# RWKV chunks of two heads: column tiles and half-array products against side-by-side operands and block-diagonal matrices on the whole array

## The chip, the cores and the metric

The kernel runs on one core of a Trainium2 chip. The metric is the device time of one execution in microseconds (us), as a median of several runs. One execution of the kernel before was profiled; every row shown below comes from it. PE is TensorE's matmul stream and PEld its weight loads, DVE is VectorE, ACT ScalarE, POOL GpSimd, and SP the engine that issues most DMAs.

## The reference, cut to what matters

Two layers, each of a mixer, a cross-attention over a memory of 256 rows, and a mixture of 16 experts, on 256 tokens of width 1024, all in f32. The change touches one half of the mixer, the RWKV-7 recurrence with 8 heads of width 64:

```python
def step(state, inp):
    r_t, w_t, k_t, v_t, kk_t, a_t = inp
    sa = jnp.einsum('bhvk,bhk->bhv', state, -kk_t)
    state = (state * w_t[:, :, None, :]
             + sa[..., None] * (kk_t * a_t)[:, :, None, :]
             + v_t[..., None] * k_t[:, :, None, :])
    return state, jnp.einsum('bhvk,bhk->bhv', state, r_t)
...
_, y = lax.scan(step, s0, (time_major(r_h), time_major(w_h), time_major(k_h),
                           time_major(v_h), time_major(kk), time_major(a_h)))
```

The other half of the mixer is a retention over 4 heads, and there are two gates; both need the products of x with columns of one large matrix `w_in`.

## The kernel before

**Chunks.** The recurrence is computed in 4 chunks of 64 tokens. Within a chunk it is a triangular system: a 64x64 matrix of each head and chunk is inverted (`invert`, all 16 of a half at once, on DVE; two levels of products on TensorE then grow 16x16 blocks to 64x64), and from chunk to chunk only the state goes on. The 8 heads lie as 4 pairs, head E of a pair on partitions 0 to 63 and head O on 64 to 127. A layer does two halves (`hf` 0 and 1) one after the other, and each half two pairs in lockstep. So there are 4 halves, 8 pairs and 32 pair-chunks in the program.

**A pair's steps** (`rwkv_pair`, a generator that gives way at each `yield`): (1) DVE and POOL write the operands `stk` (L841, L842) and `bk` (L844, L845); (2) four chunk products a head, `bk` times `stk` (L854), masked by DVE into `mb` and `stk` (L855, L856), and a DMA of the left half of `mb` to `blkin`; then the inversion; (3) the inverse `St` comes back by DMA and goes through the two levels (L876 to L892); (4) the four chunks in a row, each with three dependent stages:

```python
self.mm(pg[h, :], stk[o][:, n, 0:64], sv[o][:, n, :], True, True)
self.mm(pu[h, :], st[h, n, :], gg[h, :], True, True)
self.mm(pd[h, :], bkr[:, n, h], uv[o][:, n, :], True, True)
self.mm(pq[h, :], sv[o][:, n, :], stk[o][:, n, 64:128], True, False)
self.mm(pq[h, :], uv[o][h, n, :], mb[h, n, 64:128], False, True)
```

Each of these lines runs once for head E and once for head O. The results of the two heads go to the two partition halves of one PSUM tile, so the products with 128 rows of operands are column tiles (128x64 of the array), those with 64 rows are quadrants (64x64). DVE copies `pg` to `gg` (L919, one copy for both heads) and `pu` to `uv` (L925, one a head), makes the next state `sv` from `pd` (L932, one a head); ACT copies `pq` to `kk` (L938). Below, stretch A is the run of these four chunks in the first half of layer 0, B in its second half, C and D the same two of layer 1.

**What lies around it.** `filler` holds the products of x with `w_in` for retention and gates; `FILL` says how many of its steps are issued after each step of the pairs, none after the chunks begin. A scheduler then orders the instructions of each engine by its own model of time, so such products also stand between those of the chunks. In the trace they are `acc<-wh,xT` (512 columns) and `acc<-xT,wh` (256 columns), on the whole array. Their weights come by DMA to a ring of buffers, and are split into a high and a low part by ACT (L135) and DVE (L136). After the pairs, what is left of the filler is finished, and the outputs are projected. All matmuls go through `mm` and all transposes through `tr`, so they have L127 and L131 in the trace. An f32 matmul is two instructions there; names such as `rk<-stkE,svE` tell which operands it read, the moving one first in some rows and the stationary one in others. Tiles of one tag share its buffers: `bk` has two, one for each pair of a half.

Of the kernel before, what the change touches and what calls it, by code (L numbers as in the profile page):

```python
# [111 lines left out]
def DQ(nc):  # L112
    return nc.sync


class Build:
# [709 lines left out]
    def rwkv_pair(self, rw, pair, kk, al, k, r, v, P, Pm, Pi):  # L826
# [4 lines left out]
        def T(name, n, bufs=2):  # L831
            return rw.tile([128, 4, n], F32, name=name, bufs=bufs)
# [5 lines left out]
        stk = [T("stkE", 128), T("stkO", 128)]  # L838
        bk = T("bk", 128)
        for o, h in enumerate(half):  # L840
            nc.vector.scalar_tensor_tensor(out=stk[o][h, :, 0:64], in0=ch(kk)[h], scalar=-1.0, in1=ch(Pm)[h], op0=OP.mult, op1=OP.mult)  # L841
            nc.gpsimd.tensor_mul(out=stk[o][h, :, 64:128], in0=ch(r)[h], in1=ch(P)[h])  # L842
            b0, k0 = (0, 64) if o == 0 else (64, 0)
            nc.vector.tensor_mul(out=bk[h, :, b0:b0 + 64], in0=ch(al)[h], in1=ch(Pi)[h])  # L844
            nc.vector.tensor_mul(out=bk[h, :, k0:k0 + 64], in0=ch(k)[h], in1=ch(Pi)[h])  # L845
        yield

        mb = T("mb", 128)
        mask = c["rmask"][:, None, :].to_broadcast([128, 4, 128])
        for o, h in enumerate(half):  # L850
            x = half[1 - o]
            ps = self.rk([128, 4, 128])
            for n in range(4):
                self.mm(ps[:, n, :], bk[h, n, :], stk[o][h, n, :], True, True)  # L854
            nc.vector.tensor_mul(out=mb[h], in0=ps[h], in1=mask[h])  # L855
            nc.vector.tensor_mul(out=stk[o][x], in0=ps[x], in1=mask[x])  # L856
# [3 lines left out]
        for o, h in enumerate(half):  # L860
            DQ(nc).dma_start(out=self.matrices(self.blkin, pair, o), in_=mb[h, :, 0:64])
# [7 lines left out]
        mab = mb[:, :, 0:64]  # L869
        tm = [c["tmask"][:, None, i * 64:i * 64 + 64].to_broadcast([128, 4, 64]) for i in range(2)]  # L870
        st, tt = T("St", 64), T("Tt", 64)
        for o, h in enumerate(half):
# [5 lines left out]
        for lv in range(2):  # L878
# [13 lines left out]
            nc.vector.tensor_add(out=flat(st), in0=flat(st), in1=flat(pz[:, 0]))  # L892
            if lv == 0:
# [6 lines left out]
                uv = [T("uvE", 64), T("uvO", 64)]  # L900
                sv = [T("svE", 64), T("svO", 64)]
# [3 lines left out]
                for o, h in enumerate(half):  # L905
                    x = half[1 - o]
                    for cc in range(2):
                        nc.scalar.copy(out=uv[o][x].rearrange("p (q c) v -> p q c v", c=2)[:, :, cc, :],
                                       in_=pt[cc * 64:cc * 64 + 64, :, o * 64:o * 64 + 64])
                    nc.gpsimd.tensor_copy(out=sv[o][x], in_=uv[o][x])  # L910
                    nc.gpsimd.memset(sv[o][h, 0, :], 0.0)

        for n in range(4):
            yield
            pg = self.rk([128, 64])
            for o, h in enumerate(half):
                self.mm(pg[h, :], stk[o][:, n, 0:64], sv[o][:, n, :], True, True)
            gg = rw.tile([128, 64], F32, name="gg", bufs=2)
            nc.vector.tensor_copy(out=gg, in_=pg)  # L919
            yield  # L920
            pu = self.rk([128, 64])
            for h in half:
                self.mm(pu[h, :], st[h, n, :], gg[h, :], True, True)
            for o, h in enumerate(half):
                nc.vector.tensor_copy(out=uv[o][h, n, :], in_=pu[h])  # L925
            yield
            if n < 3:
                pd = self.rk([128, 64])
                for o, h in enumerate(half):
                    self.mm(pd[h, :], bkr[:, n, h], uv[o][:, n, :], True, True)  # L930
                for o, h in enumerate(half):
                    nc.vector.scalar_tensor_tensor(out=sv[o][h, n + 1, :], in0=sv[o][h, n, :], scalar=Pc[h, n], in1=pd[h],  # L932
                                                   op0=OP.mult, op1=OP.add)
            pq = self.rk([128, 64])
            for o, h in enumerate(half):
                self.mm(pq[h, :], sv[o][:, n, :], stk[o][:, n, 64:128], True, False)
                self.mm(pq[h, :], uv[o][h, n, :], mb[h, n, 64:128], False, True)
            nc.scalar.copy(out=kk[:, n * 64:n * 64 + 64], in_=pq)  # L938
# [426 lines left out]
```

## Time and profile before

| | |
|---|---|
| time, median of 3 runs (lowest to highest) | 1326.06 us (1325.94 to 1327.15) |
| time of the profiled execution | 1326.32 us |
| its span, first to last instruction | 1324.5 us |
| PE busy | 1225.4 us, 93% of the span |
| DVE busy | 759.1 us, 57% |
| ACT busy | 494.9 us, 37% |
| POOL busy | 73.0 us, 6% |

The time around the span is 1.8 us. Matmuls are pipelined: one that has started keeps PE "busy" until its result is out, while the next ones start behind it. What a stream of matmuls costs is read from the distance between their starts, not from their durations. In rows of busy time by stretch, the bracketed numbers are instructions, PEclk is the granted clock of TensorE as a share of 2.4 GHz, and the last two columns are the share of time in which the DMA engines moved data and their GB/s.

### The profile page before, as it was taken

Reading aid. Unit: us, or ns where it says so; the run is one execution under the profiler, and the core shown is the slowest. Engines: PE = TensorE matmul, PEld = TensorE weight load, DVE = VectorE, ACT = ScalarE, POOL = GpSimd, SP = SyncE. Lnnn points to the kernel's source line nnn. Section 1 sums busy time; section 2 is a strip of 40 time slices with the busy share of each in tenths; the row PEclk is TensorE's granted clock in tenths of the full one; section 3 lists DMA queues with packets and bytes.
Section 4 is the critical chain, followed back from the end, with each engine's and each line's share of the span. In section 5 each row is a group of like instructions: output and inputs, shape, how many; then the busy total and the mean of one; then the engine's idle time right before and its main releaser. Section 6 shows DMA issues by size and latency. Waiting matters only on the chain. (4 is left out here: it accounts for less than half of the span.)

```text
span 1324.5 us, 20023 instructions
## 1 busy us (share of the span) xinstructions
PE 1225.4 (93%) x7952; PEld 856.1 (65%) x7952; DVE 759.1 (57%) x1518; ACT 494.9 (37%) x785; POOL 73.0 (6%) x125
## 2 busy tenths in 40 slices
PE   7998998998999999999969998989979969999995
PEld 7886687796888844333329976877959854434331
DVE  6588677487557523333366787865775562333335
ACT  4556333253544322322235663332534312232222
POOL 0012221000000000000000103210000000000000
PEclk9999989999999999999989999999999979999997
DMA  9745132198834899999997452231888349999994
GB/s 318 263 148 180 50 97 76 33 323 290 276 127 175 304 398 402 398 397 402 399 341 228 159 179 72 85 96 48 302 291 312 120 166 349 402 396 401 401 396 194
DMA packets 189843, 331.10 MB, mean 250 GB/s; under 512 B 23152, under 2 KB 80880, under 8 KB 188720
## 3 DMA queue, kind: packets, MB, share of 16 engines
q1 hardware_dynamic: 187728, 324.51, 68.2%
q10 hardware_dynamic: 1728, 3.15, 0.7%
q0 software_dynamic: 288, 2.10, 0.4%
q8 instruction: 66, 1.08, 0.3%
q14 instruction: 33, 0.27, 0.1%
HBM read 321.86 MB, written 7.87 MB: 249 GB/s over the span
## 5 line engine op out<-in xcount | busy, mean ns | idle before, releaser
L136 DVE TENSOR_TENSOR wh<-raw,wh 128x1024 fp32r<-128x1024 f32 (+1 forms) x204 | 232.7, 1143 | 111.0 <-ACT wh L135 109.5
L135 ACT CAST wh<-raw 128x1024 fp32r<-128x1024 f32 (+1 forms) x204 | 199.8, 981 | 155.0 <-PE acc L127 138.5
L127 PE MATMUL acc<-xT,wh 128*128 128x256 f32 x1824 | 247.7, 289 | 2.7 <-DVE xT L136 1.6
L127 PEld LDWEIGHTS acc<-xT,wh 128*128 128x128 f32 x1824 | 225.9, 190 | 11.2 <-DVE xT L136 1.9
L1246 ACT COPY low<-g 64x512 f32<-64x512 f32 x128 | 74.2, 580 | 289.4 <-PE g L127 263.5
L127 PE MATMUL g<-raw,xe 128*64 128x512 f32 x688 | 157.7, 598 | 4.5 <-DVE hT L1255 3.4
L127 PE MATMUL acc<-wh,xT 128*128 128x512 f32 x384 | 101.9, 408 | 3.0 <-DVE vg L557 3.0
L127 PEld LDWEIGHTS g<-raw,xe 128*64 128x64 f32 x688 | 46.0, 136 | 90.7 <-issue 79.9
L1247 DVE TENSOR_TENSOR y<-g,low 64x512 f32<-64x512 f32 x64 | 44.1, 689 | 77.0 <-ACT low L1246 75.8
L127 PE MATMUL g<-raw,hT 128*64 128x512 f32 x352 | 81.4, 596 | 5.2 <-DVE hT L1255 2.6
L127 PEld LDWEIGHTS acc<-wh,xT 128*128 128x128 f32 x384 | 70.1, 188 | 21.5 <-DVE vg L557 3.8
L1247 DVE TENSOR_TENSOR us<-g,low 64x512 f32<-64x512 f32 x32 | 22.0, 689 | 94.4 <-ACT low L1246 94.3
L1247 DVE TENSOR_TENSOR act<-g,low 64x512 f32<-64x512 f32 x32 | 22.0, 689 | 75.2 <-ACT low L1246 75.1
L127 PEld LDWEIGHTS g<-raw,hT 128*64 128x64 f32 x352 | 26.1, 137 | 54.6 <-issue 41.7
L127 PE MATMUL acc<-wh,memT 128*128 128x512 f32 x192 | 51.0, 417 | 0.0
L127 PE MATMUL acc<-memT,wh 128*128 128x256 f32 x384 | 46.5, 282 | 1.6 <-DVE wh L136 1.2
L127 PEld LDWEIGHTS acc<-memT,wh 128*128 128x128 f32 x384 | 45.7, 188 | 2.6 <-DVE wh L136 1.7
L127 PE MATMUL acc<-wh,oT 128*128 128x512 f32 x192 | 45.6, 394 | 1.0 <-DVE x L406 0.8
L127 PE MATMUL acc<-wh,mT 128*128 128x512 f32 x192 | 45.7, 397 | 0.7 <-DVE xr L406 0.7
L127 PE MATMUL acc<-ys,wh 128*128 128x256 f32 x384 | 45.1, 279 | 0.0
L127 PEld LDWEIGHTS acc<-ys,wh 128*128 128x128 f32 x384 | 45.0, 188 | 0.0
L127 PEld LDWEIGHTS g<-oh,xs 128*128 128x128 f32 x256 | 33.4, 196 | 17.1 <-issue 11.2
(310 smaller groups left out, 1700.6 us busy)
## 6 DMA issues: line engine op xcount, KB each, us to landing
raw<-in_w_in_dram SPq DMA_DIRECT2D x46, 1024.0 KB, 5.1
raw<-in_moe_w_down_dram SPq DMA_DIRECT2D x44, 1024.0 KB, 14.9
raw<-in_moe_w_gate_dram SPq DMA_DIRECT2D x43, 1024.0 KB, 13.9
raw<-in_moe_w_up_dram SPq DMA_DIRECT2D x43, 1024.0 KB, 13.8
raw<-in_xa_wkv_dram SPq DMA_DIRECT2D x16, 1024.0 KB, 10.2
wh<-in_moe_w_up_dram SPq DMA_DIRECT2D x15, 1024.0 KB, 14.2
A<-in_moe_w_down_dram SPq DMA_DIRECT2D x10, 1024.0 KB, 13.6
A<-in_moe_w_gate_dram SPq DMA_DIRECT2D x9, 1024.0 KB, 13.7
```

The lines of the kernel that those rows point to most:

```text
L127: self.nc.tensor.matmul(out, lhsT, rhs, start=start, stop=stop, skip_group_check=True)
L135: self.nc.scalar.copy(out=hi, in_=src)
L136: (eng or self.nc.vector).tensor_sub(out=lo, in0=src, in1=hi)
L1246: self.nc.scalar.copy(out=low[h], in_=ps[x])
L1247: self.nc.vector.tensor_add(out=out[h], in0=ps[h], in1=low[h])
```

## The change

The operands of the two heads of a pair are laid side by side in one tile each (`stk`, `uv` and `sv` with an index for the head next to the columns). The matrices that had a block for each head in the two partition halves get a column block for each head too, with zeros in the other two blocks: `sd` (from `St`, written by the last add of the second level) and `mrb` (from the right half of `mb`; the left half is now a tile `mab` of its own). Each of the five products of a pair-chunk is then one product of 128 rows and 128 columns of operands for both heads; the blocks of the result that mix heads are not read. So the result lies in two diagonal blocks, and DVE needs two copies for `gg`, ACT two for `kk`; the last add of the second level becomes two, and the mask products of step (2) become three a head instead of two. POOL clears the zero blocks (four memsets a pair). The products of step (2) go head by head for each chunk instead of four of E and then four of O. `sd` shares the tag of `bk`, and `mrb` those of `k` and `r`.

```diff
@@ -828,37 +828,41 @@
         nc, c = self.nc, self.c
         half = [slice(0, 64), slice(64, 128)]
 
-        def T(name, n, bufs=2):
-            return rw.tile([128, 4, n], F32, name=name, bufs=bufs)
+        def T(name, n, bufs=2, tag=None):
+            return rw.tile([128, 4, n], F32, name=name, tag=tag or name, bufs=bufs)
 
         def ch(t):
             return t.rearrange("p (c t) -> p c t", c=4)
 
 
-        stk = [T("stkE", 128), T("stkO", 128)]
+        stk = rw.tile([128, 4, 2, 2, 64], F32, name="stk", bufs=2)
         bk = T("bk", 128)
         for o, h in enumerate(half):
-            nc.vector.scalar_tensor_tensor(out=stk[o][h, :, 0:64], in0=ch(kk)[h], scalar=-1.0, in1=ch(Pm)[h], op0=OP.mult, op1=OP.mult)
-            nc.gpsimd.tensor_mul(out=stk[o][h, :, 64:128], in0=ch(r)[h], in1=ch(P)[h])
+            nc.vector.scalar_tensor_tensor(out=stk[h, :, 0, o, :], in0=ch(kk)[h], scalar=-1.0, in1=ch(Pm)[h], op0=OP.mult, op1=OP.mult)
+            nc.gpsimd.tensor_mul(out=stk[h, :, 1, o, :], in0=ch(r)[h], in1=ch(P)[h])
             b0, k0 = (0, 64) if o == 0 else (64, 0)
             nc.vector.tensor_mul(out=bk[h, :, b0:b0 + 64], in0=ch(al)[h], in1=ch(Pi)[h])
             nc.vector.tensor_mul(out=bk[h, :, k0:k0 + 64], in0=ch(k)[h], in1=ch(Pi)[h])
         yield
 
-        mb = T("mb", 128)
+        mab, mrb = T("mab", 64), T("mrb", 128, 2, "kr"[pair % 2])
+        for o, h in enumerate(half):
+            nc.gpsimd.memset(mrb[h, :, half[1 - o]], 0.0)
         mask = c["rmask"][:, None, :].to_broadcast([128, 4, 128])
+        ps = [self.rk([128, 4, 2, 64]) for _ in half]
+        for n in range(4):
+            for o, h in enumerate(half):
+                self.mm(ps[o][:, n], bk[h, n, :], stk[h, n, :, o, :], True, True)
         for o, h in enumerate(half):
             x = half[1 - o]
-            ps = self.rk([128, 4, 128])
-            for n in range(4):
-                self.mm(ps[:, n, :], bk[h, n, :], stk[o][h, n, :], True, True)
-            nc.vector.tensor_mul(out=mb[h], in0=ps[h], in1=mask[h])
-            nc.vector.tensor_mul(out=stk[o][x], in0=ps[x], in1=mask[x])
+            nc.vector.tensor_mul(out=mab[h], in0=ps[o][h, :, 0], in1=mask[h, :, 0:64])
+            nc.vector.tensor_mul(out=mrb[h, :, h], in0=ps[o][h, :, 1], in1=mask[h, :, 64:128])
+            nc.vector.tensor_mul(out=stk[x, :, :, o, :], in0=ps[o][x], in1=mask[x].rearrange("p c (a t) -> p c a t", a=2))
         Pc = ch(P)[:, :, 63:64]
         bkc = T("bkc", 128, 1)
         nc.gpsimd.tensor_mul(out=bkc, in0=bk, in1=Pc.to_broadcast([128, 4, 128]))
         for o, h in enumerate(half):
-            DQ(nc).dma_start(out=self.matrices(self.blkin, pair, o), in_=mb[h, :, 0:64])
+            DQ(nc).dma_start(out=self.matrices(self.blkin, pair, o), in_=mab[h])
         yield
 
         def per(ps, lhsT, rhs):
@@ -866,9 +870,12 @@
                 for h in half:
                     self.mm(ps[h, n, :], lhsT[h, n, :], rhs[h, n, :], True, True)
 
-        mab = mb[:, :, 0:64]
         tm = [c["tmask"][:, None, i * 64:i * 64 + 64].to_broadcast([128, 4, 64]) for i in range(2)]
         st, tt = T("St", 64), T("Tt", 64)
+
+        sd = T("Sd", 128, 2, "bk")
+        for o, h in enumerate(half):
+            nc.gpsimd.memset(sd[h, :, half[1 - o]], 0.0)
         for o, h in enumerate(half):
             DQ(nc).dma_start(out=st[h], in_=self.matrices(self.blkout, pair, o))
         yield
@@ -889,53 +896,53 @@
             if lv == 0:
                 per(pz[:, 1], st, y)
                 nc.vector.tensor_add(out=flat(tt), in0=flat(tt), in1=flat(pz[:, 1]))
-            nc.vector.tensor_add(out=flat(st), in0=flat(st), in1=flat(pz[:, 0]))
-            if lv == 0:
+                nc.vector.tensor_add(out=flat(st), in0=flat(st), in1=flat(pz[:, 0]))
 
                 bkr = T("bkr", 128)
                 pt = self.rk([128, 4, 128])
                 for n in range(4):
                     self.tr(pt[:, n, :], bkc[:, n, :])
                 nc.scalar.copy(out=flat(bkr), in_=flat(pt))
-                uv = [T("uvE", 64), T("uvO", 64)]
-                sv = [T("svE", 64), T("svO", 64)]
+
+                uv, sv = (rw.tile([128, 4, 2, 64], F32, name=n, bufs=2) for n in ("uv", "sv"))
                 pt = self.rk([128, 2, 128])
                 for i in range(2):
                     self.tr(pt[:, i, :], v[:, i * 128:i * 128 + 128])
                 for o, h in enumerate(half):
                     x = half[1 - o]
                     for cc in range(2):
-                        nc.scalar.copy(out=uv[o][x].rearrange("p (q c) v -> p q c v", c=2)[:, :, cc, :],
+                        nc.scalar.copy(out=uv[x, :, o].rearrange("p (q c) v -> p q c v", c=2)[:, :, cc, :],
                                        in_=pt[cc * 64:cc * 64 + 64, :, o * 64:o * 64 + 64])
-                    nc.gpsimd.tensor_copy(out=sv[o][x], in_=uv[o][x])
-                    nc.gpsimd.memset(sv[o][h, 0, :], 0.0)
+                    nc.gpsimd.tensor_copy(out=sv[x, :, o], in_=uv[x, :, o])
+                    nc.gpsimd.memset(sv[h, 0, o], 0.0)
+            else:
+                for h in half:
+                    nc.vector.tensor_add(out=sd[h, :, h], in0=st[h], in1=pz[h, 0])
 
         for n in range(4):
             yield
-            pg = self.rk([128, 64])
-            for o, h in enumerate(half):
-                self.mm(pg[h, :], stk[o][:, n, 0:64], sv[o][:, n, :], True, True)
+            pg = self.rk([128, 128])
+            self.mm(pg, flat(stk[:, n, 0]), flat(sv[:, n]), True, True)
             gg = rw.tile([128, 64], F32, name="gg", bufs=2)
-            nc.vector.tensor_copy(out=gg, in_=pg)
+            for h in half:
+                nc.vector.tensor_copy(out=gg[h], in_=pg[h, h])
             yield
             pu = self.rk([128, 64])
-            for h in half:
-                self.mm(pu[h, :], st[h, n, :], gg[h, :], True, True)
+            self.mm(pu, sd[:, n, :], gg, True, True)
             for o, h in enumerate(half):
-                nc.vector.tensor_copy(out=uv[o][h, n, :], in_=pu[h])
+                nc.vector.tensor_copy(out=uv[h, n, o], in_=pu[h])
             yield
             if n < 3:
-                pd = self.rk([128, 64])
+                pd = self.rk([128, 128])
+                self.mm(pd, bkr[:, n, :], flat(uv[:, n]), True, True)
                 for o, h in enumerate(half):
-                    self.mm(pd[h, :], bkr[:, n, h], uv[o][:, n, :], True, True)
-                for o, h in enumerate(half):
-                    nc.vector.scalar_tensor_tensor(out=sv[o][h, n + 1, :], in0=sv[o][h, n, :], scalar=Pc[h, n], in1=pd[h],
+                    nc.vector.scalar_tensor_tensor(out=sv[h, n + 1, o], in0=sv[h, n, o], scalar=Pc[h, n], in1=pd[h, h],
                                                    op0=OP.mult, op1=OP.add)
-            pq = self.rk([128, 64])
-            for o, h in enumerate(half):
-                self.mm(pq[h, :], sv[o][:, n, :], stk[o][:, n, 64:128], True, False)
-                self.mm(pq[h, :], uv[o][h, n, :], mb[h, n, 64:128], False, True)
-            nc.scalar.copy(out=kk[:, n * 64:n * 64 + 64], in_=pq)
+            pq = self.rk([128, 128])
+            self.mm(pq, flat(sv[:, n]), flat(stk[:, n, 1]), True, False)
+            self.mm(pq, flat(uv[:, n]), mrb[:, n, :], False, True)
+            for h in half:
+                nc.scalar.copy(out=kk[h, n * 64:n * 64 + 64], in_=pq[h, h])
         yield
```

## Rows read from the trace of the kernel before

**Rows 1.** The page, part 1: busy us, share of the span, instructions.
```profile
PE 1225.4 (93%) x7952; PEld 856.1 (65%) x7952; DVE 759.1 (57%) x1518; ACT 494.9 (37%) x785; POOL 73.0 (6%) x125
```

**Rows 2.** Windows A, between, B, tail, C: length, PE, PEld, DVE, ACT, POOL, PEclk.
```profile
151.04:176.44 25.40, 25.40 (x186) 16.92 (x182) 14.43 (x45) 4.56 (x11) 5.42 (x8) 0.88 0.13 42
176.44:230.92 54.48, 50.04 (x507) 44.95 (x506) 41.84 (x133) 22.11 (x40) 9.18 (x16) 0.96 0.31 91
230.92:253.97 23.05, 23.05 (x197) 16.89 (x193) 11.38 (x40) 4.07 (x10) 0.00 (x0) 1.00 0.08 25
253.97:275.00 21.03, 21.03 (x170) 20.23 (x168) 11.73 (x23) 10.00 (x15) 0.00 (x0) 1.00 0.36 122
818.80:841.91 23.11, 23.11 (x187) 15.44 (x183) 13.21 (x44) 4.56 (x11) 4.75 (x7) 1.00 0.14 46
```

**Rows 3.** Timeline of PE inside stretch A: start us, us, instruction, count.
```profile
157.73 0.33 PE L127 MATMUL rk<-gg,St 64*64 64x64 f32 x4
158.00 0.50 PE L127 MATMUL acc<-wh,xT 128*128 128x512 f32 x1
158.43 0.33 PE L127 MATMUL rk<-gg,St 64*64 64x64 f32 x4
...
159.12 0.27 PE L127 MATMUL rk<-uvE,bkr 128*64 128x64 f32 x1
...
160.26 0.27 PE L127 MATMUL rk<-uvE,bkr 128*64 128x64 f32 x1
```

**Rows 4.** Timeline of PE elsewhere: whole-array products one after another.
```profile
113.94 10.07 PE L127 MATMUL acc<-wh,xT 128*128 128x512 f32 x42 [1.64 <-DVE vg L557]
...
182.52 1.03 PE L127 MATMUL rk<-mixc,sq 128*128 128x2 f32 x8
183.41 0.63 PE L131 MATMUL tp<-cst,rqo 128*128 128x128 f32 x4
183.80 4.83 PE L127 MATMUL acc<-xT,wh 128*128 128x256 f32 x38
...
204.14 0.91 PE L127 MATMUL acc<-vg,rst 128*128 128x128 f32 x6 [1.12 <-DVE rst L589]
```

**Rows 5.** PE groups in A, then in B: filler products among the chunks.
```profile
L127 PE MATMUL acc<-wh,xT 128*128 128x512 f32 x18 | 7.2, 461 | 0.0
L127 PE MATMUL acc<-xT,wh 128*128 128x256 f32 x12 | 4.3, 422 | 0.0
...
L127 PE MATMUL acc<-xT,wh 128*128 128x256 f32 x40 | 10.1, 334 | 0.0
```

**Rows 6.** DVE groups in B: count, busy us, mean ns, idle before.
```profile
L136 DVE TENSOR_TENSOR wh<-raw,wh 128x1024 fp32r<-128x1024 f32 x2 | 2.4, 1224 | 0.1
L925 DVE COPY uvO<-rk 64x64 f32<-64x64 f32 x8 | 1.8, 228 | 0.2
...
L932 DVE SCALAR_TENSOR_TENSOR svO<-svO,P,rk 64x64 f32<-64x64 f32 x6 | 1.7, 287 | 0.2
L919 DVE COPY gg<-rk 128x64 f32<-128x64 f32 x8 | 1.7, 221 | 5.3 <-PE rk L127 5.3
...
L892 DVE TENSOR_TENSOR St<-St,rk 128x256 f32<-128x256 f32 x2 | 0.8, 421 | 0.5 <-PE rk L127 0.5
```

**Rows 7.** Timeline, step (2) of the first half: pair products and first mask.
```profile
94.20 0.82 PE L127 MATMUL rk<-stkE,bk 64*128 64x128 f32 x5
...
96.26 0.68 DVE L855 TENSOR_TENSOR mb<-rk,mixc 64x512 f32<-64x512 f32 x1
```

**Rows 8.** Timeline: operands of the second half, before and at the end of A.
```profile
144.39 1.30 DVE L844 TENSOR_TENSOR bk<-av,cum 64x256 f32<-64x256 f32 x3
...
173.26 0.72 POOL L842 TENSOR_TENSOR stkE<-r,P 64x256 f32<-64x256 f32 x1 [6.19 <-PE rk L127]
173.33 0.93 DVE L841 SCALAR_TENSOR_TENSOR stkE<-kk,sw 64x256 f32<-64x256 f32 x1
```

**Rows 9.** ACT's group of line 938 in layer 0: busy, mean ns, idle.
```profile
L938 ACT COPY kk<-rk 128x64 f32<-128x64 f32 x16 | 3.4, 213 | 37.0 <-PE rk L127 37.0
```

## The prediction

> **What bounds the kernel now.** The page comes first: PE is busy for 93% of the span, DVE for 57% [rows 1]. That is an average, so the stretches that the change touches come next [rows 2]. In A, B and C (and D, which is B again in layer 1) PE never looks idle, and DVE is busy for about half of the time. The stretch between A and B is another matter: PE idles for 54.48 - 50.04 = 4.4 us of it and DVE is busy for 41.8 of 54.5. After B, PE is full again with filler. So what PE gives up in a chunk stretch reaches the end of the mixer, as long as the chunks' own chain does not become longer than PE's work. The weights of later stages don't hold it back: the DMA engines are busy for 0.08 to 0.36 of these stretches.
>
> Is a full PE also a useful PE? That is read from distances between starts, inside A [rows 3]. A filler product of 512 columns that stands alone between two groups of chunk products takes 158.43 - 158.00 = 0.43 us. The same product in a run of 42 takes 10.07 / 42 = 0.24 [rows 4]. So about 0.2 us is lost around each such product, at the places where the array goes from 128x128 to a tiled shape and back. The groups themselves: `pu` of one pair takes 158.00 - 157.73 = 0.27, and `pd` with `pq` 160.26 - 159.12 = 1.14 [rows 3]. `pg` looks like `pu`, so a pair-chunk costs PE 0.27 + 0.27 + 1.14 = 1.68 us, besides what the filler loses.
>
> **Step 1, the chunk products.** They become five per pair-chunk (four in the last chunk, which has no `pd`), each two instructions on the whole array: 2 pairs x (3 x 5 + 4) = 38 products, 76 instructions a stretch. No row shows these very products. Eight whole-array f32 instructions with only two moving columns, and what follows, lie 183.41 - 182.52 = 0.89 apart, so 0.111 each; six with 128 columns take 0.91 with the latency of the last one, so at most 0.15 each [rows 4]. I take 0.111: it leaves those six 0.91 - 5 x 0.111 = 0.35 for the latency of the last one, near the 0.27 of a tiled one [rows 3]. Then the products need 76 x 0.111 = 8.4 us of PE (11.4 at 0.15).
>
> The filler in B is 40 products of 256 columns [rows 5] at 4.83 / 38 = 0.127 [rows 4]: 5.1 us. In A (and C) it is 18 of 512 and 12 of 256 [rows 5]: 18 x 0.24 + 12 x 0.127 = 5.8 us. If no hand-over costs anything once all is of one shape, PE's floor is 13.5 us in B and D and 14.2 in A and C, against 23.1 now [rows 2].
>
> One rule speaks against this step. The rows show what a pair gets from tiles now: the four instructions of a `pu`, two a head, last 0.33 together, though one alone lasts 0.27 [rows 3], so the heads share the array's time. The Trainium skill, "TensorEngine Tiling (Array Packing)", section Theoretical Speedup, says the same in general: operands of at most 64 rows or columns run up to twice as fast as tiles. By it the products alone would get dearer, and the result would be that of the last rival below; by the rows above, the hand-overs that go are worth more. The sum goes by the rows.
>
> But the chunks also have a chain, and it gets longer. DVE's copies of `pg` become two; one of 64 partitions costs as much (0.228) as one of 128 (0.221) [rows 6]. For one pair-chunk DVE then works 0.45 for `gg`, 0.45 for `uv`, 0.56 for `sv`: 1.45 us, and 2.9 for both pairs. Two weight splits of 1.22 a stretch [rows 6] add 0.6 a chunk: 3.5. PE needs 2 x 10 x 0.111 + 5.1/4 = 3.5 a chunk in B, 3.7 in A. One pair alone, never disturbed, needs 3 x (0.111 + 0.35) + 1.45 = 2.8. So PE and DVE tie, and two queues that feed each other in order never both run full. I take 4.2 a chunk, 20% above the tie, and 3.4 for the last one: 16.0 a stretch. Gain 23.1 - 16.0 = 7.1, four times: 28.4 us. Bounds: 37.0 (PE's floor: 2 x 9.6 + 2 x 8.9), and 12.4 if a stretch takes 20, when most chunks wait once for a split of 1.22 on DVE.
>
> **Step 2, the clock.** A holds the same work as C but takes 25.40 against 23.11; the granted clock there is a mean 0.88, in C 1.00 [rows 2]: part of A ran at 1.2 GHz. Whether a denser PE keeps 2.4 GHz is open: 0 to 2.3 us, taken 1.1 gain.
>
> **Step 3, step (2) of the pairs.** The first mask product starts 96.26 - 94.20 = 2.06 us after the first pair product [rows 7]. With E and O alternating, on different rows of the array and different PSUM tiles, sixteen instructions of a pair may overlap two by two: 8 x 0.111 + 0.27 = 1.2, so 0.9 earlier a half; or not at all. The mask products go from four of 0.68 to six (0.43, 0.43, 0.69 a head): +0.36 a pair, 0.7 a half. Both bounds, four halves: -3.6 to +2.9; taken 0.
>
> **Step 4, the evictions that become two.** `sd`: one add of 0.42 [rows 6] becomes two of about 0.42, eight pairs: 3.4 us, before the first `gg` in DVE's queue but beside `pg` and filler on PE: half, +1.7 (0 to 3.4). `kk`: 32 more copies of 0.21 on ACT, which idles for 37.0 us in layer 0 alone before such copies [rows 9]: hidden, but for the last of each half: +0.4 (0 to 0.8). POOL's 32 memsets lie on an engine that is busy for 73 us in all [rows 1]; nothing waits for them but `mrb` and `sd`, whose inputs come later. `uv` and `sv` are written by as many instructions as before, and the DMAs stay two a pair, each of the same size.
>
> **Step 5, a wait that is new.** `sd` lies in the buffers of `bk`, and is read until the last `pu` of a half. Now the second half's `bk` is written before A starts, at 144.4 [rows 8]. After the change it can't be before A's last `pu`: 8 products of 0.43 a layer, 3.5 us, go to the end of A, where the second half's `stk` (L841) already waits its turn at 173.3. DVE's product took 0.93 there beside one of POOL's [rows 8], so up to 8 x 0.93 = 7.4. What queues behind are the pair products and the inversion. PE's cover is `rwkv_out` and filler; DVE has none, since it is busy three quarters of that stretch. Taken +2 a layer: +4 (0 to 14.8). `mrb` in the buffers of `k` and `r` waits for readers of step (1) only, which stand ahead of it in DVE's and POOL's queues: nothing.
>
> **The sum.** -28.4 - 1.1 + 0 + 1.7 + 0.4 + 4 = -23.4. The profiled execution took 1326.3 (span 1324.5 and 1.8 around it): 1302.9. It lies 0.3 above the median of 1326.06: **1302.6 us**.
>
> **Rivals.**
> *PE alone sets the pace.* The scheduler's order happens to keep DVE ahead. For it: A and B now hold one filler product between most groups, which is time in which DVE can finish; against it: DVE is as full as PE. 1326.0 - 37.0 - 1.1 + 1.7 + 0.4 + 0 to 4 = 1290 to 1294; with the clock and step 3 in full, 1285.
> *DVE and the chain set the pace.* A split of 1.22 in front of a copy delays both pairs, and a stretch takes 20: 1326.0 - 12.4 - 1.1 + 6.1 = 1318.6, and 1322 with half of step 5's bound. For it: DVE idles only 5.3 us before `gg` in B [rows 6], and DVE's work grows.
> *It all comes back between A and B.* Step 5 at its bound (14.8) with that last case: 1326.0 - 12.4 - 1.1 + 2.1 + 14.8 = 1329, or no change when the filler covers a part. For it: PE already idles there.
> *Slower: packing is lost and nothing else.* Suppose the 0.2 us around a filler product has to do with waiting for operands, not with the shape. Then the distances of 0.43 stay, and only the array's time grows. The four instructions of a `pu` start within at least 0.33 - 0.27 = 0.06 us of each other [rows 3]; taken as 0.1, a whole-array product of 0.222 costs 0.12 more: 38 x 0.12 = 4.6 a stretch, 18 in all: 1326.0 + 18 + 6 = 1350. It decides from the point where a lone filler product still takes over 0.4. Against it: from eight f32 instructions to four transposes to filler, all on the whole array, nothing of the kind shows (183.80 - 183.41 = 0.39 for four) [rows 4].
> The Trainium skill, "TensorEngine Tiling (Array Packing)", speaks on both sides of this last rival: section Key Properties says that a change of the tiling mode, not merely of the tile, drains TensorE, and the 0.43 against 0.24 agrees; section Theoretical Speedup is weighed in step 1.
>
> **How the numbers follow.** Forecast (1296 to 1312) 0.54; PE's floor 0.18; DVE's pace 0.14; given back 0.05; packing lost 0.09. 0.2% (2.7 us) is about what a measurement of this kernel can tell from no change. The first three are faster: 0.86; same 0.05; slower 0.09. The range leaves out most of the last two and the far ends of both faster rivals: 1285 to 1320.
>
> **What would show it.** Right: chunk products `128*128`, 0.11 apart; lone filler products at 0.24; A to D near 16 us, with PE waiting for `gg` and `uv` at times and DVE above 80%. Steps 3 and 5: the first mask about 1.2 us after the first pair product, and the second half's `bk` behind A's last `pu`, with the inversion no more than 2 us later after A's end than now. Wrong: distances of 0.4 around filler; a product that costs 0.15 or more; PE idle for over a fifth of a chunk stretch; or the stretch between A and B longer by what A got shorter.

## The result and the profile after

The changed kernel takes 1311.76 us (median of four, 1307.25 to 1320.17), the kernel before 1326.61 beside it: ratio 0.987, interval 0.9825 to 0.9915. Beside the experiments the same kernel before took 1321.95 to 1346.91 us, so medians that lie a few us apart say little. The profiled execution is the fastest of the four: 1307.25 us with a span of 1305.5, 19.0 less than that of before. The page, part 1, answers to [rows 1]: 304 PE instructions fewer, DVE 10.6 us busier, POOL 8.9.

```profile
PE 1199.3 (92%) x7648; PEld 850.1 (65%) x7648; DVE 769.7 (59%) x1574; ACT 500.1 (38%) x817; POOL 81.9 (6%) x157
```

Where the 19.0 us came from is read from windows: first the changed kernel's stretches A, between, B, and C, between, D (columns as in [rows 2]), then the last two of the kernel before, which [rows 2] don't hold.

```profile
147.10:166.00 18.90, 18.00 (x121) 14.88 (x118) 17.46 (x58) 7.12 (x20) 5.50 (x8) 1.00 0.17 57
166.00:225.70 59.70, 51.70 (x498) 46.87 (x496) 45.44 (x142) 20.92 (x39) 13.63 (x25) 0.91 0.29 83
225.70:242.60 16.90, 16.52 (x134) 15.60 (x131) 14.29 (x50) 5.17 (x17) 0.00 (x0) 1.00 0.11 32
...
805.49:824.37 18.88, 18.00 (x121) 14.89 (x118) 17.44 (x58) 7.12 (x20) 5.50 (x8) 1.00 0.18 57
824.37:884.61 60.24, 51.91 (x497) 47.03 (x496) 45.42 (x142) 20.91 (x39) 13.63 (x25) 0.92 0.28 82
884.61:901.52 16.91, 16.52 (x134) 15.63 (x131) 14.28 (x50) 5.17 (x17) 0.00 (x0) 1.00 0.27 93
```

```profile
841.91:896.40 54.49, 49.65 (x508) 45.03 (x506) 42.83 (x134) 22.10 (x40) 9.77 (x17) 0.97 0.31 91
896.40:919.45 23.05, 23.05 (x197) 16.89 (x193) 11.38 (x40) 4.07 (x10) 0.00 (x0) 1.00 0.22 70
```

The four chunk stretches lost 6.5, 6.2, 4.2 and 6.1 us: 23.0. The stretches between them grew by 5.2 and 5.8: 11.0 given back. A starts 3.9 us earlier; from B's end to C's start is 1.9 shorter, from D's end to the last instruction 1.1. Sum: -23.0 + 11.0 - 6.9 = -19.0. So 6.9 us come from outside the stretches that the change touches, and no run gives a cause for them; in a second profile of the same kernel (E8) it is 3.0. The two first halves won almost nothing: from A's start to B's start it is 78.6 us (79.9 before), from C's to D's 79.1 (77.6).

The stretches are better than they look, because more filler fits into them. The groups of PE in A, then in B, of the changed kernel (answering to [rows 5]):

```profile
L127 PE MATMUL acc<-wh,xT 128*128 128x512 f32 x18 | 6.1, 433 | 0.0
L127 PE MATMUL acc<-xT,wh 128*128 128x256 f32 x15 | 3.7, 324 | 0.0
L131 PE MATMUL tp<-cst,rqo 128*128 128x128 f32 x8 | 1.6, 280 | 0.0
...
L127 PE MATMUL acc<-xT,wh 128*128 128x256 f32 x54 | 10.0, 303 | 0.0
```

Filler priced as in step 1 (0.24, 0.127, a transpose 0.111) is 7.1 us of A and 6.9 of B. What is left for the chunks: A 18.9 - 7.1 = 11.8 (25.4 - 5.8 = 19.6 before), B 10.0 (18.0 before). The gain at equal work is 7.8 in A, 7.9 in B and D, and 5.4 in C.

The timeline of PE in B shows why. From one `pu` to the next there are two filler products, and 0.46 us: 0.22 and 2 x 0.12, nothing lost.

```profile
236.11 0.33 PE L127 MATMUL rk<-gg,Sd 128*128 128x64 f32 x2
236.25 0.48 PE L127 MATMUL acc<-xT,wh 128*128 128x256 f32 x2
236.57 0.39 PE L127 MATMUL rk<-gg,Sd 128*128 128x64 f32 x2
...
238.04 0.39 PE L127 MATMUL rk<-stk,sv 128*128 128x128 f32 x2
238.27 0.39 PE L127 MATMUL rk<-mrb,uv 128*128 128x128 f32 x2
```

The chunk products behind them lie 238.27 - 238.04 = 0.23 apart, 0.11 an instruction. In A, where the lone product of 512 columns took 0.43 [rows 3], the same reading gives 0.32 (0.24 in a run), and 0.53 with the chunk product ahead of it:

```profile
153.10 0.46 PE L127 MATMUL rk<-sv,stk 128*128 128x128 f32 x2
153.31 0.48 PE L127 MATMUL acc<-wh,xT 128*128 128x512 f32 x1
153.63 0.33 PE L127 MATMUL rk<-gg,Sd 128*128 128x64 f32 x2
```

The 0.08 us that is left there is a wait for an operand: DVE ends the copy to `gg` at 153.44, 0.19 before the `pu`. It is the same in B, where the three filler products that still stand alone take 0.28, 0.35 and 0.35, and the chunk product behind each starts 0.15 after DVE's write of its operand. In the kernel before it was not so: the twelve that stand alone in B take 0.31 to 0.32 each, and for ten of them the operand of the product behind had been written 0.6 to 2.0 us earlier.

What came back after A is in the timelines of the changed kernel from 164 to 187 us: DVE, then POOL, then PE (bracket: idle before it, and on what).

```profile
164.61 0.42 DVE L844 TENSOR_TENSOR bk<-av,cum 64x256 f32<-64x256 f32 x1
...
165.90 0.95 DVE L845 TENSOR_TENSOR bk<-k,cum 64x256 f32<-64x256 f32 x1
...
167.22 0.94 DVE L844 TENSOR_TENSOR bk<-av,cum 64x256 f32<-64x256 f32 x1
168.09 0.95 DVE L845 TENSOR_TENSOR bk<-k,cum 64x256 f32<-64x256 f32 x1
...
169.41 0.41 DVE L844 TENSOR_TENSOR bk<-av,cum 64x256 f32<-64x256 f32 x1
...
171.72 0.42 DVE L845 TENSOR_TENSOR bk<-k,cum 64x256 f32<-64x256 f32 x1
172.17 0.69 DVE L781 SCALAR_TENSOR_TENSOR kk<-rk,kk 128x512 f32<-128x512 f32 x1
...
184.49 1.22 DVE L136 TENSOR_TENSOR wh<-raw,wh 128x1024 fp32r<-128x1024 f32 x1 [3.65 <-ACT wh L135]
```

```profile
164.97 1.60 POOL L842 TENSOR_TENSOR stk<-r,P 64x256 f32<-64x256 f32 x2 [4.38 <-PE rk L127]
...
167.01 1.75 POOL L842 TENSOR_TENSOR stk<-r,P 64x256 f32<-64x256 f32 x2
168.70 0.99 POOL L850 MEMSET mrb<- 64x256 f32 x3
```

```profile
167.61 0.48 PE L127 MATMUL rk<-stk,bk 64*128 64x128 f32 x2
169.19 2.24 PE L127 MATMUL rk<-stk,bk 64*128 64x128 f32 x22 [1.09 <-DVE bk L845]
173.01 2.04 PE L127 MATMUL rk<-stk,bk 64*128 64x128 f32 x8 [1.58 <-DVE kk L781]
```

`bk` is now written from 164.6 to 172.1, at the end of A and behind it; before, it was written from 144.4 on, ahead of A [rows 8]. Three of its eight products take twice as long as the others, those beside POOL's products for `stk`. PE stops twice in the middle of the pair products. At 181 DVE stops too, behind a weight split that waits for ACT, though the matrices of the inversion have landed by 182.1 (loaded from 179.7, 2.4 us to landing); the inversion starts at 186.25, 20.3 us after A's end (before: at 190.90, 14.5 after it).

### The profile page after: what moved, and what is told of

Its sections match the earlier page's. It is cut to its first block, busy times and chain, and to the rows that moved or that the text cites. A ratio compares the mean times of both kernels' runs of the same rounds, so it can differ in the third digit from the quotient of the medians.

```text
span 1305.5 us, 19592 instructions
## 1 busy us (share of the span) xinstructions
PE 1199.3 (92%) x7648; PEld 850.1 (65%) x7648; DVE 769.7 (59%) x1574; ACT 500.1 (38%) x817; POOL 81.9 (6%) x157
## 5 line engine op out<-in xcount | busy, mean ns | idle before, releaser
L127 PEld LDWEIGHTS acc<-wh,xT 128*128 128x128 f32 x384 | 70.2, 188 | 19.6 <-DVE vg L557 3.5
```

What stands on the lines that cost most here:

```text
L127: self.nc.tensor.matmul(out, lhsT, rhs, start=start, stop=stop, skip_group_check=True)
```

## The experiments

Each run stands beside runs of the kernel before on its own chip. Distances are from the one profile of each. A chunk stretch goes from the start of its first chunk product to the end of its last.

**E1, `sd` in another buffer** (on the changed kernel).

```diff
-        sd = T("Sd", 128, 2, "bk")
+        sd = T("Sd", 128, self.nq, "q")
```

> One edit to the changed kernel: the block-diagonal sd lies in buffers of the tag q, which are dead by then, and no longer in those of bk; so the second half's bk can be written before the first half's chunks again. Theory 1 (the wait of step 5): it accounts for most of the 5.8 us (layer 0) and 7.4 us (layer 1) by which the time from the end of a first half's chunks to the start of the inversion grew, so about 10 us come back: near 1301 us, pair products of the second half starting within 3 us of the end of the chunks and lasting about 2 us instead of 7. Rival: that time is lost anyway, because stk has to wait for the last pq, POOL's products and memsets stand beside DVE's, and less filler is left; then within 3 us of the changed kernel, 1309 to 1313.

1302.51 us, ratio 0.9778 (0.9725 to 0.9832), as the theory has it. The pair products of the second half run without a stop, and the stretches between are 55.89 and 54.18 us instead of 59.70 and 60.24. Timeline of PE, and windows of A, between A and B, C and D:

```profile
169.53 2.53 PE L127 MATMUL rk<-stk,bk 64*128 64x128 f32 x32
```

```profile
148.22:167.92 19.70, 18.83 (x128) 15.73 (x125) 18.23 (x58) 7.12 (x20) 6.30 (x8) 1.00 0.18 55
167.92:223.81 55.89, 50.51 (x491) 45.66 (x489) 41.52 (x134) 20.90 (x39) 8.92 (x18) 0.91 0.31 88
...
826.05:880.23 54.18, 48.80 (x490) 44.06 (x488) 41.52 (x134) 20.90 (x39) 8.92 (x18) 0.94 0.32 91
```

A and C are 0.8 longer than in the changed kernel, for PE does seven more filler products ahead of their last chunk product. So the whole way is compared: from A's start to B's it is 75.59 us (78.60), from C's to D's 73.90 (79.12). The wait of step 5 costs 3.0 + 5.2 = 8.2 us. But the inversion starts 18.9 and 17.4 us after A's and C's end (20.3 and 20.4 in the changed kernel, 14.5 and 13.0 in the kernel before): the wait is only 1.3 and 3.0 of the 5.8 and 7.4 by which the inversion had moved, and in this the theory falls.

Why the last chunk product of A comes late is in DVE's timeline: a weight split stands ahead of the last copies to `uv`, and the product that reads them starts at 167.48.

```profile
165.72 1.23 DVE L136 TENSOR_TENSOR wh<-raw,wh 128x1024 fp32r<-128x1024 f32 x1
166.96 0.46 DVE L933 COPY uv<-rk 64x64 f32<-64x64 f32 x2
```

**E2, only `pu` as two 64x64 quadrants again** (on the changed kernel), from `St`; so there is no `sd`, no second add and no wait.

```diff
-            self.mm(pu, sd[:, n, :], gg, True, True)
+            for h in half:
+                self.mm(pu[h, :], st[h, n, :], gg[h, :], True, True)
```

> The changed kernel with pu alone as before: two 64x64 quadrants from St, and so no sd, no second add, no memsets for it and no wait on bk. Theory 1 (hand-overs come from the change of the array's shape): each pu group lies about 0.27 us from the next instruction and the filler product around it takes about 0.2 longer than in a run; 8 groups a stretch, about 2 us a stretch, 8 in all, against 10 to 13 us back from the wait on bk and 1.7 from the add: 1305 to 1309. Rival (hand-overs are waits for operands): the groups cost what they cost on the whole array, and the time falls by the wait alone, to about 1299.

1316.47 us, ratio 0.9877 (0.9806 to 0.9948): above both ranges, and 14.0 slower than E1, though the wait is gone from both. Its timeline of PE in B shows lone filler products among the quadrants:

```profile
235.02 0.38 PE L127 MATMUL acc<-xT,wh 128*128 128x256 f32 x1
235.33 0.33 PE L127 MATMUL rk<-gg,St 64*64 64x64 f32 x2
235.59 0.38 PE L127 MATMUL acc<-xT,wh 128*128 128x256 f32 x1
```

A filler product takes 235.33 - 235.02 = 0.31 there, as in the kernel before, and 0.12 among whole-array products: the hand-over came back with the shape, 0.19 us each. B is 1.9 us longer than in the changed kernel with 15 filler products fewer, 3.8 at equal work; A is 0.3 longer at equal work. With C and D that makes 8.2 us, the 8 that the theory had for the groups. What it did not have is in the stretches between: 63.55 and 60.32 us, at a granted clock of 0.87 and 0.92 (E1: 0.91 and 0.94). By (1 - clock) x length that is 13.1 us lost there, and 8.3 in E1. The clock so accounts for most of the rest, as an estimate; why it is lower here is open.

**E3, no alternation** (the changed kernel with its pair products head after head), and **E4, alternation alone** (the kernel before with only that).

```diff
-        for n in range(4):
-            for o, h in enumerate(half):
+        for o, h in enumerate(half):
+            for n in range(4):
                 self.mm(ps[o][:, n], bk[h, n, :], stk[h, n, :, o, :], True, True)
```

> The changed kernel with the pair products in the order of before (four of E, then four of O). Theory 1 (alternating heads overlap on different rows of the array): pair products of the first half take about 2.6 us again instead of 1.8, the first mask product comes up to 0.8 us later in each of four halves: 0 to 3 us slower, 1312 to 1315. Rival (the overlap is reached in either order, or DVE is late anyway): no change within 1 us.

> The kernel before with nothing but the pair products alternating between the heads. Theory 1: pair products of the first half in 1.8 us instead of 2.6, and 1 to 3 us less in all, 1323 to 1325. Rival: no change (1326), since DVE has other work at that time.

E3 1311.57 us, ratio 0.9841 (0.9769 to 0.9912), as the changed kernel's (and 9.1 above E1, which ran beside it); E4 1335.93, ratio 1.0016 (0.9969 to 1.0063). The first half's pair products, first start to last, take 1.78 us alternating and 2.55 head after head, in either kernel; the time shows nothing of it.

**E5, the wait alone** on the kernel before.

```diff
+        sc = rw.tile([128, 4, 128], F32, name="Sc", tag="bk", bufs=2)
...
-            nc.vector.tensor_add(out=flat(st), in0=flat(st), in1=flat(pz[:, 0]))
+            nc.vector.tensor_add(out=sc[:, :, 0:64] if lv else st, in0=st, in1=pz[:, 0])
...
-                self.mm(pu[h, :], st[h, n, :], gg[h, :], True, True)
+                self.mm(pu[h, :], sc[h, n, 0:64], gg[h, :], True, True)
```

> The kernel before, with one thing of the change: the last inverse (the 64 columns that the second add of the second level writes) goes to a tile in the buffers of bk, and pu reads it there. Nothing else of the change: shapes, copies and products are those of before. The wait of step 5 stands alone. Theory (the wait gives back what the shorter chunk stretch gains): the second half's bk can't be written before the last pu of A; eight products of 0.42 to 0.94 us and the pair products behind them come later, and the second half's chunks start 3 to 7 us later after A's end than in the kernel before, in each layer: 6 to 14 us in all, about 1333 to 1340 beside 1326. Rival (the give-back is only PE working at half clock and DVE's queue, and the wait is covered): the distance from A's end to the second half's chunks stays within 1.5 us of that of before, and so does the time, within 0.3%.

1348.61 us, ratio 1.0122 (1.0078 to 1.0166): 17.5 slower, above the theory's range. Windows between A and B, C and D:

```profile
173.00:237.37 64.37, 57.38 (x506) 52.01 (x505) 47.54 (x142) 21.81 (x40) 11.97 (x18) 0.87 0.27 77
...
851.50:916.36 64.86, 58.75 (x507) 52.91 (x506) 46.58 (x140) 21.90 (x40) 11.06 (x15) 0.83 0.27 76
```

They grew from 54.5 to 64.4 and 64.9, by 9.9 and 10.4, with PE idle for 7.0 and 6.1 us and a granted clock of 0.87 and 0.83 (0.96 and 0.97 before). By (1 - clock) x length 15.6 of these 20.3 us are PE at 1.2 GHz, so what the wait holds up by itself is some 5 us. That the wait brings the low clock is not shown: E4, without it, runs B at 0.76 (28.34 us instead of 23.05).

**E6, half of the copies on ACT** (on E1).

```diff
-                nc.vector.tensor_copy(out=gg[h], in_=pg[h, h])
+            nc.vector.tensor_copy(out=gg[half[0]], in_=pg[half[0], half[0]])
+            nc.scalar.copy(out=gg[half[1]], in_=pg[half[1], half[1]])
```

and the same for `uv`.

> The changed kernel with sd in a buffer of its own, and with the second copy of gg and the second copy of uv of each pair-chunk done by ACT, no longer by DVE. Theory (after the change DVE sets the pace of the chunk stretches: it is busy for 17.5 of 18.9 us in A, 14.3 of 16.9 in B): DVE loses 16 copies of 0.22 us a stretch, 3.5 us, and A to D become 1.5 to 3 us shorter each: about 1294 to 1298 beside 1302.5 with sd's own buffer alone. Rival (the chain and PE, with 16.5 to 18 us of their own, set the pace, and a copy that queues behind one of ACT's weight casts comes later than on DVE): the stretches stay within 1 us, the time within 2 us, or 2 to 6 us longer.

1298.70 us, ratio 0.9735 (0.965 to 0.982). Windows A, between, B:

```profile
148.75:166.74 17.99, 17.65 (x125) 15.34 (x122) 13.99 (x42) 9.91 (x36) 6.67 (x7) 1.00 0.18 60
166.74:220.79 54.05, 48.45 (x493) 43.48 (x491) 40.28 (x134) 20.78 (x39) 9.32 (x19) 0.94 0.33 91
220.79:237.91 17.12, 17.03 (x136) 15.73 (x133) 10.43 (x34) 8.36 (x32) 0.00 (x0) 1.00 0.11 32
```

DVE lost 4.2 us of A (18.23 in E1) and 3.8 of B. A and C became 1.7 us shorter (18.00 in C), 1.3 at equal work; B and D became 0.2 longer. So in A and C DVE holds the chunks up, as the theory has it (at the low end of its 1.5 to 3 us), and in B and D it does not. From A's start to B's it is 72.04 us (75.59 in E1), from C's to D's 72.28 (73.90). The time is 0.7 above the theory's range, and its interval overlaps that of E1. DVE reaches the second half's operands earlier, too: its first product for `stk` starts at 166.06, in E1 at 167.45, and the inversion 15.8 us after A's and C's end, in E1 18.9 and 17.4.

**E7, the filler later** (on E1): two filler steps go from beside the second half's pair products to beside the inversion.

```diff
-        (1,) * 2 + (3,) * 6 + (1,) * 4 + (0,) * 14)
+        (0,) * 2 + (4,) * 2 + (3,) * 4 + (1,) * 4 + (0,) * 14)
```

> The changed kernel with sd in a buffer of its own; the two filler steps that were issued beside the second half's pair products, one for each of its first two steps, come two steps later, beside the inversion. Theory (the second half's inversion starts some 20 us after A's end because DVE's queue holds a weight split of the filler, which waits for ACT's cast, which stands behind a gate that waits for PE's filler): without that filler ahead of it the inversion starts at least 3 us earlier after A's end, in both layers, and the second half's chunks 2 to 6 us earlier; the time is 1292 to 1300. Rival (what is late is the operands and the mask products themselves, and the filler is needed to keep PE at work there): the inversion starts within 1.5 us of where it did, PE idles longer, and the time is 1302 to 1308.

1301.48 us, ratio 0.9757 (0.9678 to 0.9836). From the start of the last chunk product of A, and of C, to the inversion it is 17.6 and 19.2 us (E1: 19.2 and 17.6): 1.5 earlier in one layer and 1.5 later in the other, as the granted clock between the halves, 0.94 and 0.91 (E1: 0.91 and 0.94). The theory falls for this edit.

**E8, the changed kernel again.**

> The changed kernel itself once more, beside the others of this call. Theory and rival agree: 1305 to 1314, with A to D at 17 to 19 us and the second half's pair products spread over some 7 us after A's end. How far its profile moves from the first one of the same kernel is the yardstick for the others.

1314.59 us, ratio 0.9837 (0.9755 to 0.9919), 0.6 above the range. Windows between A and B, C and D:

```profile
168.56:231.37 62.81, 54.63 (x497) 49.52 (x495) 45.48 (x142) 20.93 (x39) 13.67 (x25) 0.86 0.28 79
...
830.50:893.55 63.05, 54.74 (x497) 49.64 (x495) 45.49 (x142) 20.93 (x39) 13.67 (x25) 0.86 0.28 78
```

The same instructions, the same DVE time, and 3 us longer each than in the first profile, at a granted clock of 0.86 instead of 0.91. A and B are within 0.03 us of the first profile. So the runs of one kernel differ by the clock behind A, and with this profile as the yardstick the wait costs 6.1 + 8.0 = 14.1 us instead of 8.2 (81.71 and 81.95 us from A's start to B's and C's to D's, against E1).

**E9, the two products of `pq` twice** (on E1), off the chain.

```diff
-            self.mm(pq, flat(sv[:, n]), flat(stk[:, n, 1]), True, False)
-            self.mm(pq, flat(uv[:, n]), mrb[:, n, :], False, True)
+            for _ in range(2):
+                self.mm(pq, flat(sv[:, n]), flat(stk[:, n, 1]), True, False)
+                self.mm(pq, flat(uv[:, n]), mrb[:, n, :], False, True)
```

> The changed kernel with sd in a buffer of its own, and with the two products of pq done twice for each pair-chunk, the first time for nothing: 16 products (32 instructions) more a stretch, which nothing waits for but the copies to kk that nobody waits for either. Theory (since taking 3.5 us of copies off DVE shortened the stretches by at most 0.5 us, PE sets their pace): 32 x 0.112 = 3.6 us more in each of the four stretches, 14 in all, about 1314 to 1319. Rival (the chain from stage to stage and DVE set the pace and PE has room): the stretches grow by 0 to 1.2 us each, 1302 to 1307.

1307.74 us, ratio 0.9857 (0.9765 to 0.9949). Windows A and B:

```profile
148.75:169.74 20.99, 19.29 (x144) 17.41 (x141) 18.97 (x58) 6.53 (x19) 5.44 (x7) 1.00 0.16 51
...
224.15:242.43 18.28, 17.80 (x150) 17.19 (x147) 13.52 (x50) 5.42 (x17) 0.00 (x0) 1.00 0.09 30
```

The time is 0.7 above the rival's range and far below the theory's. All four stretches are 1.3 us longer than in E1, but A holds some 15 filler products of 256 and 2 transposes fewer (2.1 us), B some 16 (2.0): 3.4 and 3.3 at equal work, where 3.6 of PE were added. So PE had no room for them, and the theory is right on the pace: the stretches pay for nearly all the work of PE that is put in. The premise of the expectation is wrong for A and C, where E6's copies are worth 1.7. The span rose by only 6.1 us over E1's 1300.6, not by 14: the stretches between took up the displaced filler and came out at 54.41 and 54.43 us (55.89 and 54.18 in E1), at a granted clock of 0.97 (0.91 and 0.94).

**E10, a third buffer for `stk`** (on E6; its other lines are those of E1 and E6), and **E11, E6 with the filler of E7**.

```diff
-            self.nraw, self.nhi, self.nq = 3, 3, 8
+            self.nraw, self.nhi, self.nq = 3, 3, 7
...
-        stk = rw.tile([128, 4, 2, 2, 64], F32, name="stk", bufs=2)
+        stk = rw.tile([128, 4, 2, 2, 64], F32, name="stk", bufs=3)
```

> The kernel with ACT's share of the copies and sd in a buffer of its own, with a third buffer for stk (paid for with one of the eight buffers of the group that sd uses). Two of the four DVE products that write the second half's stk can be made before A, as bk's are. Theory (what DVE still has to do between A's last copy and the mask products is on the path to the second half's chunks): 1.3 to 1.9 us less between A and B, and between C and D, 1294 to 1296. Rival (the inversion's start is set by something later, the roots of rwkv_out and the weight splits in DVE's queue): the distance stays within 0.7 us, 1297 to 1300.

> The kernel with ACT's share of the copies and sd in a buffer of its own, and with the two filler steps beside the second half's pair products moved two steps later. Theory (the two edits act at different places: the copies free DVE at the end of A, the later filler frees it before the inversion): another 1.5 us a layer, 1293 to 1297. Rival (once DVE is free earlier, the filler is what fills PE there, and its absence costs what it saves): 1297 to 1302.

E10 1300.20 us, ratio 0.9775 (0.9701 to 0.9849); E11 1298.92, ratio 0.9783 (0.9715 to 0.985). From the last chunk product of A to the first of B it is 54.4 and 54.6 us (E6: 54.3): both rivals hold. In E10 DVE has two products fewer to do there, and waits 1.10 us for PE in their place. E6 has the lowest ratio of all; it is 15.9 us below the changed kernel that ran beside it (E8) and 32.4 below the kernel before. From E1, E7, E10 and E11 the intervals don't separate it.

## Why the prediction was right, and where its terms were off

The sign and the mechanism were right. The time is 9.2 us above the forecast of 1302.6, and 0.2 below the upper end of the range. That it lies inside is in part luck: of the 19.0 us in the profile 6.9 lie outside the stretches that the sum priced (3.0 in E8's profile), while the terms of the sum brought -23.0 + 11.0 = -12.0 where -23.4 was forecast.

**Step 1 was right, and so nearly was its size.** Chunk products lie 0.112 apart, as taken. At equal work the stretches gained 5.4 in C, as much in A without the clock (next step), and 7.9 in B and D each: 26.6 us, forecast 28.4. The tie of PE and DVE held in A and C alone: there both more work of PE (E9) and less of DVE (E6) move the length, by 3.4 and 1.3 us at equal work. In B and D PE alone sets the pace. The stretches stay above PE's floor with the filler they hold (8.4 + 7.1 = 15.5 in A, 8.4 + 6.9 = 15.3 in B) by 3.4 and 1.6 us.

**The slower rival (packing lost) falls.** E2 is its test: with quadrants a lone filler product takes 0.31, with whole-array products 0.12. The 0.19 us between them is the shape's: the operands behind such products had long been written in the kernel before, and where a lone one still takes 0.28 to 0.35 in the changed kernel, a wait for DVE ends it. The Trainium skill, "TensorEngine Tiling (Array Packing)", section Key Properties, has the rule (a change of the tiling mode drains TensorE), and the trace agrees; by its section Theoretical Speedup alone `pu` would be cheaper as quadrants, and E2 shows it dearer where filler stands between.

**Step 2: the clock was won in A and lost behind it.** A and C now take the same 18.9 us, so A won the whole 2.3 that it took longer than C (its bound; 1.1 forecast). That the denser PE won it is not shown: E4 and E5, with the chunk products of before, run A in 23.14 us at a granted clock of 1.00. And the granted clock between A and B fell from 0.96 to 0.91. (1 - clock) x length, for A and the stretch after it together, is 3.0 + 2.2 before and 0 + 5.4 after.

**Step 3: nothing, as taken, but not as told.** The first mask product was to start 1.2 us after the first pair product. It starts 3.2 after, for DVE's queue holds three weight splits ahead of it (timeline of PE, then DVE, in the first half):

```profile
93.81 2.06 PE L127 MATMUL rk<-stk,bk 64*128 64x128 f32 x32
```

```profile
93.60 3.50 DVE L136 TENSOR_TENSOR wh<-raw,wh 128x1024 fp32r<-128x1024 f32 x3
97.01 0.41 DVE L858 TENSOR_TENSOR mab<-rk,mixc 64x256 f32<-64x256 f32 x1
```

E3 and E4 show that the 0.8 us which alternation saves on PE goes nowhere.

**Step 4 was sized from the right row**: DVE's adds for `sd` take 0.418 each, and its copies of `pg` 0.222 (groups of DVE in B). Neither these adds nor ACT's copies to `kk` were tried alone.

```profile
L928 DVE COPY gg<-rk 64x64 f32<-64x64 f32 x16 | 3.6, 222 | 0.6 <-PE rk L127 0.2
...
L920 DVE TENSOR_TENSOR Sd<-St,rk 64x256 f32<-64x256 f32 x4 | 1.7, 418 | 0.5 <-PE rk L127 0.5
```

**Step 5 was the mis-sized term, and the clock is the larger part of what it missed.** The wait was found, with its place, its instructions and their 0.93 us; it was priced at +2 a layer, 4 in all, and 11.0 us were given back. E1 puts 8.2 to 14.1 us on the wait (against the two profiles of the changed kernel); its bound was 14.8. How much of that is PE at 1.2 GHz can be estimated by (1 - clock) x length of the two stretches between: 3.8 us before, 10.2 and 17.6 in the changed kernel's two profiles, 8.3 in E1, 19.4 in E5. Two profiles of one kernel bear the measure out: 62.81 us at 0.86 and 59.70 at 0.91, 3.1 apart, where it gives 3.4. At an equal clock, then, 4.6 of the 11.0 us were given back, and the wait's own price is 5 to 6 us against E1 and 5 in E5. That is near the 4 of the sum. The other 6.4 are the clock behind A, which the sum put at nothing. No run holds the clock still, so what lowers it stays open.

DVE's work has the same size: from A's start to B's DVE is busy for 62.9 us in the changed kernel and 59.8 in E1, and the same from C's to D's, 6.2 in all. The cover that was named, `rwkv_out` and filler on PE, did not hide it: PE sat idle for 8.0 us between A and B (4.4 before, 5.4 in E1). The sign that the inversion would come no more than 2 us later after A's end failed, with 5.8 and 7.4. In the trace ACT's gate (L536) waits for filler, ACT's cast for the gate, DVE's split at 184.49 for the cast, and the inversion stands behind the split. But this chain is not the wait's: E1 has it as well (gate at 180.09, split at 181.66), and E7, which moved filler away, gained nothing. Half of the copies on ACT (E6) bring the inversion to 15.8 us after A's end. Timeline of ACT:

```profile
182.92 0.60 ACT L536 ACTIVATE x<-acc 128x512 f32<-128x512 f32 x1 [2.21 <-PE acc L127]
183.42 1.04 ACT L135 CAST wh<-raw 128x1024 fp32r<-128x1024 f32 x1
```

With the 11.0 us given back in place of 4 the sum of the prediction becomes 1309.6; the median is 1311.8.

**Of the rivals**, "PE alone sets the pace" was right on the engine in B and D, and too good on the time. "DVE and the chain" was right in kind for A and C, where a split does stand ahead of copies (E1) and the stretch takes 18.9 to 19.7, near its 20; B and D took 16.9. "It all comes back between A and B" was right on the place, for the first halves alone: A's and C's gain came back, B's and D's did not. In layer 1 that is the prediction's own sign of being wrong, 5.8 us longer between C and D for 4.2 shorter in C; layer 0 has 5.2 for 6.5. Behind B and D PE finds filler enough, as [rows 2] showed for the tail.

## What to carry to other kernels

When a queue alternates between matmuls of two shapes, look at what a lone product of the other stream costs there; if it is near twice its price in a run, bring all to one shape, even at the price of zero blocks. A new tile's tag is part of the change: ask what the old owner of the buffer wrote early, for that early write is what goes. Work that moves behind a stretch costs time in the queue of its own engine; here filler on another engine did not hide it. And put the clock of the stretch behind into the sum as well: here, by the estimate of step 5, it took back as much as the wait itself.

## What the runs showed of the hardware

DVE's product of two SBUF operands (64x256) takes 0.42 us alone and 0.95 beside one of POOL's, as the rows of `bk` and POOL above show; beside POOL's memsets (168.70 to 169.69) it keeps its 0.41. The Trainium skill, "SBUF — State Buffer", section SBUF: two separate sides, says that a DVE instruction with two SBUF inputs and a GpSimd one that reads SBUF take turns on a shared port, for the whole instruction; the trace agrees that the two hold each other up and that memsets do not, while it is too coarse to show the turns. Two f32 products on different rows of the array start as little as 0.01 us apart when they alternate (E4), and the 32 pair products, 2.55 us head after head, take 1.78.
